# A two-layer mLSTM and attention step on one core: other places for weight sums, norm squares, row masks, sample queries and a last state

## The chip, the cores and the metric

The kernel runs on one core of a Trainium2 chip. Its time is the device time of one execution in microseconds (us), and of several runs the median counts. The engines are named PE (TensorE), DVE (VectorE), ACT (ScalarE), POOL (GpSimd) and SP (SyncE, which only issues DMAs here).

## The reference

One inference step of a decoder of two layers over 16 meta rows and 1024 prompt rows, and over 8 samples of 8 rows, with the same weights. Layer 0 mixes by an mLSTM recurrence (8 heads, chunks), layer 1 by an attention with forget gates that reads one shared K and V (for the samples, 4 pages of cache each as well). Cut to what matters:

```python
def run_trunk(h, C0, n0, m0, lead, attend, prm):
    for l in range(2):
        if l == 0:
            a, (C, n, m) = mlstm_mixer(rmsnorm(h, norm_a), C0, n0, m0, lead, w_in_a, ..., w_out_a)
        else:
            a = fox_mixer(rmsnorm(h, norm_b), shared, attend, w_qo_b, q_norm_b, w_out_b)
        h = h + a
        h = h + swiglu(rmsnorm(h, norm_ffn[l]), w_gate_up[l], w_down[l])
        if l == 0:
            shared = shared_kv(h, norm_kv, w_kvf, b_fg_b, k_norm_b)   # k, v, log forget values
    return rmsnorm(h, norm_final), C, n, m, shared

def mlstm_mixer(...):          # p = xn @ w_in: q, k, v, output gate, two gate columns a head
    lf = log_sigmoid(softcap(gf + b_fg))
    h, state = mlstm_sequence(q, k, v, li, lf, state0, lead)         # C: 64x128 a head, n: 64
    return (rmsnorm(h, mh_g) * sigmoid(og)) @ w_out, state

def swiglu(xn, w_gu, w_d):     # D_FF = 2816
    gu = xn @ w_gu
    return (silu(gu[..., :D_FF]) * gu[..., D_FF:]) @ w_d
```

The outputs are y of both groups, the last C, n and m, and the new k, v and log forget values. D_MODEL is 1024 and everything is float32.

## The kernel before

The 1104 rows (80 of samples and meta rows, 1024 of the prompt) lie along the free dimension in four pieces (TS, 276 rows each) or three (TT: 336, 384, 384); the model dimension lies on the partitions, in 8 blocks (KT). A float32 product is three fp32r products of a high and a low part (`mm3`, L189 to L191). The high part is a cast on ACT, the low part a difference on DVE: L261 and L262, or L255 and L256 where a gain is multiplied in, L249 and L250 in the first phase.

The program runs in this order. **phase_a** makes queries, keys, values and gates of the mLSTM. In its loop over the query and key products (mmA), the gates' log-sigmoid is taken (a chain of DVE steps, L269 to L280) and turned by TensorE (rps, L880, from lf_tm); stg holds a product until it is stored to qkD, and wo_out splits w_out into whi and wlo and stores them to woD. **The recurrence** goes over 9 chunks; behind the last, `last_state` stores C and n (out_p_C, out_p_n) and `norm_heads` takes the heads' norm from squares that ACT sums up (jk, L1228). **mlp** of layer 0 makes the output projection in units (pops, L512; `unit(t, m, x)` does 128 columns for row piece t), among which `gate` turns the normed heads and multiplies them by the output gates loaded from ogD (ghps and ogc, L1314 and L1315). **ffn** makes gate and up products of pairs of column blocks by a seven-product scheme (m1 to m7 of 2x2 blocks; L1369 the products, L1350 and L1375 the additions that combine them). `PairWeights` makes the weights' sums (L82 to L85) and splits them, `TwoNorms` the row pieces' sums and their high and low parts (T?A_ and T?B_, L104). The down projection (dps, L1701) follows in rounds, with the row pieces' norms for what comes next. **first_values** and **phase_b** make K, V, the forget values and the layer 1 queries (tmps, bps, btp); `attend_sample`, `attend_prompt`, **mlp** of layer 1 and the last norm follow.

A norm of a row piece is made in four steps. `square` (ACT, L328) adds block after block into sq, on POOL or, for the last ones, on DVE (L333). `root` sums over the partitions on TensorE (nps, L341) and takes the root on ACT (L344). `diag` takes the reciprocal and puts it on a diagonal (DVE, L350 and L352). `spread` multiplies by ones on TensorE (nps, L359) and copies out on ACT (L360). The products of the last blocks are in the list of sums and not in one tile.

What sets the order: on the engines named in a `manual_schedule` instructions run as the program writes them, on the others a tile scheduler places them. PE is fixed in the query and key loop; PE, DVE, ACT and POOL in the recurrence; PE, DVE and ACT from output unit 1 on, through the start of ffn up to `order.close()`; PE, DVE and ACT in the loop over the later column blocks; PE alone in the down projection and the sample attention. phase_b is placed by the scheduler. `Q` is a list of jobs with a cost each; `tick(x)` runs the next ones for x us of room, `tick(99)` all of them:

```python
def go(x, h, *names):
    for y in names:
        getattr(x, y)(h)           # the product
        getattr(x, y + "_out")(h)  # its additions
        tick(1.0)
```

A tile is taken from a pool under a tag; a tag has one or more buffers, and the next tile of a tag waits until the oldest is free. jk of the recurrence has two, and so have bhi and blo (the high and low parts of the turned queries, stored to qDh and qDl). The sample attention (`turn`: ktp, kT; `score`: sps, from kT and the block-diagonal queries qb) begins while output gates (bps, og2D) are still made. qmt are the meta rows' queries, built in the same way (L2319 and L2323). Row masks (L2113 to L2118) are 128 partitions by 8 or 16 columns, NEG away from a diagonal of blocks: POOL sets and cuts the copies in a scratch tile (tag rm, one buffer), DVE takes their maximum (qi and q8, mi and m16).

Of the kernel before, what the change touches and what calls it, by code (L numbers as in the profile page):

```python
# [17 lines left out]
P = 128  # L18
D = 1024
# [74 lines left out]
class TwoNorms:  # L94
# [69 lines left out]
    def jobs(self):  # L164

        return [(2.0, lambda: self.scaled(range(4))), (2.0, lambda: self.scaled(range(4, 8))), (1.3, self.first),
                (1.3, self.second_a), (1.5, self.second_b), (1.3, self.second_c), (1.5, self.second_d)]

    def late_jobs(self):
        return [(1.5, self.third), (1.3, self.third_b), (1.3, self.fourth), (1.3, self.fifth)]  # L170


class Net:
# [19 lines left out]
    def consts(self):  # L193
# [12 lines left out]
        self.clast = c.tile([P, 1], F32, name="clast")  # L206
        with self.pool("g0") as gp, self.pool("g0p", space=PSUM) as pp:
# [85 lines left out]
    def tm_proj(self, pieces, g, pp, tag, bufs, evac, then=None):  # L293
# [3 lines left out]
        parts = [  # L297
            self.load_w([p[a * P : b * P] for p in pieces], None if g is None else g + a, nk=b - a)
            for a, b in zip(ks, ks[1:])
        ]  # L300
# [17 lines left out]
    def add_sq(self, H, t, m, sp, x, late=KT - 1):  # L318
# [3 lines left out]
        n = t1 - t0  # L322
        if x == 0:
# [91 lines left out]
    def run(self):  # L415
# [4 lines left out]
        self.Q = []  # L420
# [30 lines left out]
    def mlp(self, H, raws, w, l, heads=None, cb=None):  # L451
# [5 lines left out]
        with self.pool(self.uid("nsp")) as sp, self.pool(self.uid("npp"), bufs=2, space=PSUM) as pn:  # L457
# [14 lines left out]
            with ExitStack() as c:  # L472
# [60 lines left out]
                for m in range(KT):  # L533
                    unit(0, m, m)
                    gate(1) or gate(2)
# [111 lines left out]
def phase_a(self, vt):  # L647
# [5 lines left out]
    with ExitStack() as c3:  # L653
# [59 lines left out]
        with self.pool("rowsA") as rp, self.pool("rowsAp", bufs=2, space=PSUM) as rpp, \  # L713
# [220 lines left out]
def recurrence(self, kp, rec, v, qkD, fill, gate):  # L934
# [12 lines left out]
    with ExitStack() as cr, self.pool("recAp", bufs=2, space=PSUM) as pp:  # L947
# [28 lines left out]
        with self.pool("rec2") as sets[2], self.pool("rec1", bufs=2) as rp, self.pool("rec3") as sets[0]:  # L976
# [8 lines left out]
            for i in range(1, NT):  # L985
# [11 lines left out]
                if i == NT - 1:  # L997
                    self.last_state(C[i % 2])
# [21 lines left out]
def last_state(self, C):  # L1020
# [300 lines left out]
def ffn(self, H, l, weights, order, TA, pn, pair, each, early, end=None):  # L1321
# [14 lines left out]
    with self.pool(f"ffn{l}") as fp, self.pool(f"ffnp{l}", space=PSUM) as pp:  # L1336
# [197 lines left out]
        Q += [(1.3, lambda: weights.split(1, 0, a1)), (2.2, lambda: weights.sums(1, nc.vector))]  # L1534
# [3 lines left out]
        n.diag()  # L1538
        go(g, 0, "m7")
# [12 lines left out]
        n.third()  # L1552
# [3 lines left out]
        n.third_b()  # L1556
# [7 lines left out]
        weights.split_sums(1, 0)  # L1564
        weights.sums(2)
# [9 lines left out]

        weights.split(2, 0)
        u.do("m7", "m5")
# [222 lines left out]
def first_values(self, H, pp, pn):  # L1800
# [3 lines left out]
    halves = self.vhalves  # L1804
    for tiles in ((0, 1), (5,), (2, 3), (4,), (6, 7), (8,)):
        vs = self.ny(f"vf{tiles[0]}").rearrange("p k t -> p (k t)")[:, :512].rearrange("p (i d) -> p i d", i=2)
        for z, i in enumerate(tiles):
# [14 lines left out]
            elif i == 1:  # L1822
                self.diag(st)
                self.tick(2.0)
# [869 lines left out]
```

## Time and profile before

| | |
|---|---|
| time, median of 3 runs | 2888.94 us (2888.35 to 2890.04) |
| profiled execution | 2890.53 us: a span of 2887.8 us and 2.7 us around it |
| mean granted TensorE clock | 0.988 |
| busy | PE 97%, PEld 93%, DVE 61%, ACT 40%, POOL 29% of the span |
| DMA | 469.42 MB, mean 163 GB/s |

Times in views of the trace count from the start of the span. A row of the timeline has the start, the busy time (of a group of like instructions, with xcount), the engine, the line, the operation, the tile written and the tiles read, and in brackets the idle time ahead of it with what ended it. A row of the waits has the waiting engine, its line and tile, what it waited for, and then the total in us, the number of times and the longest. A row of the stretches has from and to, the length, the busy time of PE, PEld, DVE, ACT and POOL each with its number of instructions, the granted clock (1.00 is full), the DMA engines' busy share and GB/s.

### The profile page before, as it was taken

What the parts mean: (1) busy time and instruction counts of PE and PEld (TensorE: products, weight loads), DVE (VectorE), ACT (ScalarE), POOL (GpSimd) and SP (SyncE); (2) the same over time, 40 slices, a digit from 0 to 9 for tenths busy, and PEclk for the clock granted to TensorE, in tenths of its full rate; (3) what the DMA queues carried; (4) which work ended last, traced back from release to release, by engine and by line L of the source; (5) the groups of instructions that cost most, each with busy time, mean ns of one, the idle gap of its engine ahead of it and who ended that gap; (6) DMA issues with size and microseconds to landing.
All of it is one profiled execution on the core that took longest, in us unless ns stands there. A gap on an engine that the chain in (4) does not pass through costs nothing. (4 is left out here: it accounts for less than half of the span.)

```text
span 2887.8 us, 60472 instructions
## 1 busy us (share of the span) xinstructions
PE 2789.8 (97%) x23601; PEld 2674.4 (93%) x23601; DVE 1773.3 (61%) x3905; ACT 1166.5 (40%) x2288; POOL 836.3 (29%) x1299
## 2 busy tenths in 40 slices
PE   7999989999999999999999999999999999999998
PEld 7999879999999999998999888777899999999998
DVE  5142555788887656563354443677468888866557
ACT  5232463433232334343344454777433232333345
POOL 2021233223233322124353201445332232232111
PEclk9999999999999999999999999999999999999999
DMA  6374546245555375544444676444423555526557
GB/s 197 103 220 124 144 142 229 74 132 166 176 164 158 105 233 176 182 152 132 130 165 139 200 279 238 162 138 134 139 75 104 176 162 175 171 83 220 188 190 227
DMA packets 427255, 469.42 MB, mean 163 GB/s; under 512 B 42114, under 2 KB 352506, under 8 KB 425946
## 3 DMA queue, kind: packets, MB, share of 16 engines
q1 hardware_dynamic: 380066, 317.04, 35.4%
q0 software_dynamic: 44496, 147.07, 15.8%
q8 instruction: 185, 3.03, 0.4%
q10 hardware_dynamic: 2408, 1.46, 0.2%
q14 instruction: 100, 0.82, 0.1%
HBM read 318.25 MB, written 147.21 MB: 161 GB/s over the span
## 5 line engine op out<-in xcount | busy, mean ns | idle before, releaser
L1369 PE MATMUL m<-xh,slot 128*128 128x276 f32 x2752 | 540.6, 290 | 1.2 <-ACT fs L1398 1.2
L1369 PEld LDWEIGHTS m<-xh,slot 128*128 128x128 f32 x2752 | 439.5, 188 | 3.2 <-ACT fs L1398 1.9
L1369 PE MATMUL m<-xl,slot 128*128 128x276 f32 x1376 | 397.2, 289 | 0.2
L1369 PEld LDWEIGHTS m<-xl,slot 128*128 128x128 f32 x1376 | 258.7, 188 | 0.6 <-DVE xl L104 0.6
L190 PE MATMUL tmps<-slot,xh 128*128 128x256 f32 (+2 forms) x864 | 243.4, 282 | 4.5 <-DVE slot L256 4.5
L189 PE MATMUL tmps<-slot,xh 128*128 128x256 f32 (+2 forms) x864 | 245.9, 285 | 0.0
L191 PE MATMUL tmps<-slot,xl 128*128 128x256 f32 (+2 forms) x864 | 243.3, 282 | 0.0
L262 DVE TENSOR_TENSOR slot<-slot,slot 128x1024 fp32r<-128x1024 f32 x124 | 162.7, 1313 | 62.7 <-ACT slot L261 61.2
L261 ACT CAST slot<-slot 128x1024 fp32r<-128x1024 f32 x124 | 129.5, 1045 | 130.0 <-PE m L1369 109.8
L190 PEld LDWEIGHTS tmps<-slot,xh 128*128 128x128 f32 (+1 forms) x864 | 160.6, 186 | 5.0 <-DVE slot L256 4.7
L191 PEld LDWEIGHTS tmps<-slot,xl 128*128 128x128 f32 (+1 forms) x864 | 160.9, 186 | 0.0
L189 PEld LDWEIGHTS tmps<-slot,xh 128*128 128x128 f32 (+1 forms) x864 | 160.1, 185 | 0.2
L189 PE MATMUL mmA<-xh,whi 128*128 128x384 f32 (+1 forms) x384 | 134.1, 349 | 0.1
L191 PE MATMUL mmA<-xh,wlo 128*128 128x384 f32 (+1 forms) x384 | 127.2, 331 | 0.0
L190 PE MATMUL mmA<-xl,whi 128*128 128x384 f32 (+1 forms) x384 | 127.2, 331 | 0.0
L262 DVE TENSOR_TENSOR slot<-vA,slot 128x1024 fp32r<-128x1024 f32 (+1 forms) x59 | 81.5, 1385 | 33.9 <-ACT slot L261 32.8
L262 DVE TENSOR_TENSOR slot<-Ht,slot 128x1024 fp32r<-128x1024 f32 (+1 forms) x59 | 81.3, 1380 | 33.9 <-ACT slot L261 32.8
L250 DVE TENSOR_TENSOR wlo<-wraw,whi 128x1024 fp32r<-128x1024 f32 (+1 forms) x32 | 39.0, 1226 | 100.5 <-ACT whi L249 76.9
L261 ACT CAST slot<-vA 128x1024 fp32r<-128x1024 f32 (+1 forms) x59 | 60.8, 1035 | 97.9 <-PE m L1369 92.1
L261 ACT CAST slot<-Ht 128x1024 fp32r<-128x1024 f32 (+1 forms) x59 | 60.8, 1036 | 97.7 <-PE m L1369 91.5
L1473 DVE TENSOR_TENSOR ws<-ws 128x128 f32<-128x128 f32 x264 | 93.7, 355 | 8.9
L2516 ACT ACTIVATE s<-s,nb 128x272 f32<-128x272 f32 (+7 forms) x126 | 98.8, 786 | 0.0
(755 smaller groups left out, 8711.7 us busy)
## 6 DMA issues: line engine op xcount, KB each, us to landing
ws<-in_w_down SPq DMA_DIRECT2D x176, 128.0 KB
sD<-ws SPq DMA_DIRECT2D x176, 128.0 KB
slot<-sD SPq DMA_DIRECT2D x40, 512.0 KB
slot<-in_w_gate_up SPq DMA_DIRECT2D x36, 512.0 KB
kp<-in_cache_k SPq DMA_DIRECT2D x32, 512.0 KB
vp<-in_cache_v SPq DMA_DIRECT2D x32, 512.0 KB
vA<-in_w_gate_up SPq DMA_DIRECT2D x26, 512.0 KB
Ht<-in_w_gate_up SPq DMA_DIRECT2D x26, 512.0 KB
```

The source lines that it names most:

```text
L189: mm(ps, sh, mh, start=first, stop=False)
L190: mm(ps, sh, ml, start=False, stop=False)
L191: mm(ps, sl, mh, start=False, stop=last)
L250: low = lambda: nc.vector.tensor_tensor(out=lo, in0=raw, in1=hi.bitcast(F32), op=ALU.subtract)
L261: self.nc.scalar.copy(hi, src)
L262: self.nc.vector.tensor_tensor(out=lo, in0=src, in1=hi.bitcast(F32), op=ALU.subtract)
L1369: nc.tensor.matmul(u.ps[h, b], w[p][:, k], x[q][:, k], start=first and k == i == 0, stop=k == 3 and i == 2, skip_group_check=True)
L1473: tt(out=o, in0=a, in1=b, op=ALU.subtract)
L2516: nc.scalar.activation(ss[z, u], ss[z, u], AF.Exp, bias=nb[:, z : z + 1], accum_out=sm[:, u, z : z + 1])
```

## The change

- **Weight sums behind the diagonal.** In `ffn`, the sums of the second pair of weights are queued behind `n.diag()`; the steps third_a and third_b of `TwoNorms` become jobs, and what is left comes in another order; the splits and sums of later weights stand behind the products m7 and m5 of the next unit.
- **Squares added one step later.** The DVE addition of a square is kept in `owed` until the next square or the root.
- **Row masks early.** Both masks are made in the query and key loop of phase_a, into one constant tile, rowm.
- **Third weight part early.** The third part of the last value columns' weights is made among the row tiles 6 and 7 of `first_values`.
- **Sample queries at once.** qtS and ktS are loaded on POOL's queue right behind the last store of qS and kS; all block-diagonal copies are DVE's; og0s (the first output gates) moves from the buffer of whi to one of bhi.
- **Last state turned.** n is copied (nnP), transposed by TensorE (nnpP), copied again (noP) and stored in rows; in the first output unit, the number of gates at each of the eight steps goes from one each to 0, 1, 1, 1, 2, 1, 1, 1.

```diff
class TwoNorms:
-    def third(self):
+    def third_a(self):
         for z, t in enumerate(self.t2):
             ks = slice(4 + 2 * z, 6 + 2 * z)
             self.sub(self.y1[:, ks], self.y1[:, ks], t)
-        self.net.nc.scalar.copy(self.T[4][0], self.y1[:, self.hi])
...
+    def third_c(self):
+        self.net.nc.scalar.copy(self.T[4][0], self.y1[:, self.hi])
...
         return [(2.0, lambda: self.scaled(range(4))), (2.0, lambda: self.scaled(range(4, 8))), (1.3, self.first),
-                (1.3, self.second_a), (1.5, self.second_b), (1.3, self.second_c), (1.5, self.second_d)]
+                (1.3, self.second_a), (1.5, self.second_b), (1.3, self.second_c), (1.5, self.second_d),
+                (1.5, self.third_a), (1.3, self.third_b)]
 
     def late_jobs(self):
-        return [(1.5, self.third), (1.3, self.third_b), (1.3, self.fourth), (1.3, self.fifth)]
+        return [(0.0, self.third_c), (1.3, self.fifth), (1.3, self.fourth)]

Net.consts:
+        rm = c.tile([P, P], F32, name="rowm")
+        self.q8, self.m16 = rm[:, :NQ], rm[:, NQ : NQ + NM]

Net.tm_proj (the weight parts are made by the new tm_weights, as functions):
+    def tm_proj(self, pieces, g, pp, tag, bufs, evac, then=None, parts=()):
+        ks, todo = self.tm_weights(pieces, g)
+        parts = [*parts, *(f() for f in todo[len(parts) :])]

Net.square and Net.root:
+        self.settle()
...
-        (nc.vector if x >= late else nc.gpsimd).tensor_tensor(out=s, in0=s, in1=sq, op=ALU.add)
+        if x >= late:
+            self.owed.append(lambda: nc.vector.tensor_tensor(out=s, in0=s, in1=sq, op=ALU.add))
+        else:
+            nc.gpsimd.tensor_tensor(out=s, in0=s, in1=sq, op=ALU.add)
+
+    def settle(self):
+        while self.owed:
+            self.owed.pop()()
 
     def root(self, t, pp, **kw):
+        self.settle()

mlp, first output unit:
                     unit(0, m, m)
-                    gate(1) or gate(2)
+                    for _ in range((0, 1, 1, 1, 2, 1, 1, 1)[m]):
+                        gate(1) or gate(2)

phase_a, loop over the query and key products:
+                if x == 12:
+                    for n, out in ((NQ, self.q8), (NM, self.m16)):
+                        self.row_mask(rp.tile([P, P // n, n], F32, name=self.uid("rm"), tag="rm"), out, n)

last_state:
-        nc.gpsimd.dma_start(O["p_n"][0, 0, a::2].rearrange("j k -> k j").unsqueeze(2), cs[:, :, DV:])
+    n = rp.tile([P, DV], F32, name="nnP", tag="jk")
+    nc.vector.tensor_copy(n[:, :4], C[:, :, DV])
+    ps = pp.tile([P, P], F32, name="nnpP", tag="cps")
+    nc.tensor.transpose(ps[:4, :], n[:, :4], self.ident)
+    no = rp.tile([P, DV], F32, name="noP", tag="jk")
+    nc.vector.tensor_copy(no[:4], ps[:4])
+    nc.gpsimd.dma_start(O["p_n"][0, 0].rearrange("(j a) k -> j a k", a=2), no[:4].rearrange("p (a k) -> p a k", a=2))

ffn:
-        Q += [(1.3, lambda: weights.split(1, 0, a1)), (2.2, lambda: weights.sums(1, nc.vector))]
+        Q += [(1.3, lambda: weights.split(1, 0, a1))]
         go(g, 0, "m1", "m6")
         n.root()
         go(g, 0, "m2")
         n.diag()
+        Q += [(2.2, lambda: weights.sums(1, nc.vector))]
...
         g.m7(1)
-        n.third()
+        n.third_c()
         g.m6(1)
         g.m6_out(1)
         g.m7_out(1)
-        n.third_b()
         n.fourth()
...
         go(g, 1, "m3")
-        weights.split_sums(1, 0)
-        weights.sums(2)
         weights.load(3)
...
+        u.do("m7")
+        weights.split_sums(1, 0)
+        weights.sums(2)
+        u.do("m5")
         weights.split(2, 0)
-        u.do("m7", "m5")

first_values:
+    todo, self.v3 = self.tm_weights([self.I["w_kvf"][:, D + 768 : D + 1040]], G_KV)[1], []
...
+            elif i in (6, 7):
+                self.v3.append(todo.pop(0)())

phase_b (and parts=self.v3 in the call of tm_proj for c == 3):
+        self.qkS = [sk.tile([P, 8, T0], F32, name=n) for n in ("qtS", "ktS")]
...
                             nc.gpsimd.dma_start(dstS[f], st)
+                            if f == 7:
+                                nc.gpsimd.dma_start(self.qkS[1 - gi], dstS.rearrange("m p t -> p m t"))
...
-        s = w7.tile([P, KT * P], F32R, name="og0s", tag="whi", bufs=1).bitcast(F32)
+        s = fp.tile([P, GL], F32R, name="og0s", tag="bhi").bitcast(F32)

attend_sample (its two row masks and its loads of qtS and ktS are gone):
-                (nc.vector if b else nc.gpsimd).tensor_copy(Q[r, u::2, c : c + NQ], qt[r, u::2, b * NQ : (b + 1) * NQ])
+                nc.vector.tensor_copy(Q[r, u::2, c : c + NQ], qt[r, u::2, b * NQ : (b + 1) * NQ])
```

The change moves instructions at many places; here are three on VectorE. The lines in the rows of the kernel after are its own, up to 36 higher than before's for the same step.

In the query and key loop of phase_a (lsz, lsq and lsw belong to the log-sigmoid), VectorE before:

```order
L271 TENSOR_SCALAR lsz_1945<-lse_1944 128x72
L272 RECIPROCAL lsz_1945<-lsz_1945 128x72
L273 TENSOR_TENSOR lsz_1945<-lsz_1945,lse_1944 128x72
L274 TENSOR_TENSOR lsq_1946<-lsz_1945 128x72
L275 TENSOR_SCALAR lsw_1947<-lsq_1946 128x72
```

And after:

```order
L276 TENSOR_SCALAR lsz_1946<-lse_1945 128x72
L2151 TENSOR_REDUCE rowm<-rm_2488 128x8
L277 RECIPROCAL lsz_1946<-lsz_1946 128x72
L2151 TENSOR_REDUCE rowm<-rm_2602 128x16
L278 TENSOR_TENSOR lsz_1946<-lsz_1946,lse_1945 128x72
L279 TENSOR_TENSOR lsq_1947<-lsz_1946 128x72
```

Both masks' reduces now stand between two steps of the chain that ends in lf_tm.

In the start of layer 0's ffn (ws are the down weights' sums, fs and vA products and normed rows), VectorE before, from the second T0B part on:

```order
L104 TENSOR_TENSOR T0B_2l<-t_383_6138,T0B_2h 128x552
L1350 TENSOR_TENSOR ws_0_6291<-ws_0_6291 128x128
L1473 TENSOR_TENSOR ws_0_6291<-ws_0_6291 128x128 x3
L1375 TENSOR_TENSOR vA<-m_385_6158,vA 128x276
L104 TENSOR_TENSOR vA<-vA,t_382_6137 128x552
L104 TENSOR_TENSOR vA<-vA,t_383_6138 128x552
L1350 TENSOR_TENSOR fs_5978<-fs_5978,m_387_6218 128x276
L1350 TENSOR_TENSOR vA<-fs_5978,m_386_6202 128x276
L104 TENSOR_TENSOR T0B_1l<-vA,T0B_1h 128x1104
L104 TENSOR_TENSOR T0B_4l<-vA,T0B_4h 128x1104
```

And after:

```order
L104 TENSOR_TENSOR T0B_2l<-t_385_6316,T0B_2h 128x552
L104 TENSOR_TENSOR vA<-vA,t_384_6315 128x552
L104 TENSOR_TENSOR vA<-vA,t_385_6316 128x552
L1378 TENSOR_TENSOR ws_0_6463<-ws_0_6463 128x128
L1501 TENSOR_TENSOR ws_0_6463<-ws_0_6463 128x128 x2
L1403 TENSOR_TENSOR vA<-m_387_6336,vA 128x276
L104 TENSOR_TENSOR T0B_1l<-vA,T0B_1h 128x1104
L1501 TENSOR_TENSOR ws_0_6463<-ws_0_6463 128x128
L1378 TENSOR_TENSOR ws_1_6466<-ws_1_6466 128x128
L1501 TENSOR_TENSOR ws_1_6466<-ws_1_6466 128x128 x3
L1378 TENSOR_TENSOR fs_6156<-fs_6156,m_389_6397 128x276
L104 TENSOR_TENSOR T0B_4l<-vA,T0B_4h 128x1104
```

T0B_1l moves up by two additions of products; T0B_4l moves behind the sums of the down weights of both blocks.

At the start of the sample attention, VectorE before, from the last blo of the queries on:

```order
L1959 SCALAR_TENSOR_TENSOR blo_18236<-btp_18231,gqk,bhi_18235 128x384
L256 SCALAR_TENSOR_TENSOR wlo_19405<-slot_4749,gain,whi_19404 128x128 x8
L2201 COPY kT_18263<-ktp_18307 128x512
L2201 COPY kT_18264<-ktp_18326 128x512
L2190 COPY qb_14780<-qtS 64x4x8 x4
L2323 COPY qmt_20196<-qtS 64x16 x8
```

And after:

```order
L2217 COPY qb_14786<-qtS 64x4x8 x4
L261 SCALAR_TENSOR_TENSOR slot_4934<-slot_4926,gain,slot_4930 128x128 x8
L261 SCALAR_TENSOR_TENSOR wlo_19409<-slot_4927,gain,whi_19408 128x128 x2
L1993 SCALAR_TENSOR_TENSOR blo_18234<-btp_18229,gqk,bhi_18233 128x384
L261 SCALAR_TENSOR_TENSOR wlo_19409<-slot_4927,gain,whi_19408 128x128 x6
L1993 SCALAR_TENSOR_TENSOR blo_18244<-btp_18239,gqk,bhi_18243 128x384
L2350 COPY qmt_20200<-qtS 64x16 x8
L2228 COPY kT_18267<-ktp_18311 128x512
L2228 COPY kT_18268<-ktp_18330 128x512
```

The qb copies and the split of wlo move ahead of the last blo, and the qmt copies ahead of the first kT.

More of the change, by code (lines that the diff above doesn't have):

```diff
@@ L291, in fm_cols, with tm_weights @@
             self.mm3(ps, wh[:, k, :], wl[:, k, :], xh[:, k, :], xl[:, k, :], k == 0, k == KT - 1)
-    def tm_proj(self, pieces, g, pp, tag, bufs, evac, then=None):
+    def tm_weights(self, pieces, g):
         n = sum(p.shape[1] for p in pieces)
         ks = (0, 4, 8) if n <= 256 or not self.slots else (0, 3, 6, 8)
[L297 to L300, printed above, removed]
+        make = lambda a, b: self.load_w([p[a * P : b * P] for p in pieces], None if g is None else g + a, nk=b - a)
+        return ks, [(lambda a=a, b=b: make(a, b)) for a, b in zip(ks, ks[1:])]
+    def tm_proj(self, pieces, g, pp, tag, bufs, evac, then=None, parts=()):
+        n = sum(p.shape[1] for p in pieces)
+        ks, todo = self.tm_weights(pieces, g)
+        parts = [*parts, *(f() for f in todo[len(parts) :])]
         at = [(w, k) for w, a, b in zip(parts, ks, ks[1:]) for k in range(b - a)]
@@ L419, in run @@
         self.slots = None
-        self.Q = []
+        self.Q, self.owed = [], []
         cy, cb = ExitStack(), ExitStack()
@@ L2098, in sample_prep @@
     nc.gpsimd.memset(ncn, NEG)
-    q8 = sp.tile([P, NQ], F32, name="q8")
-    qi = sp.tile([P, HB, NQ], F32, name="qi", tag="rm")
-    self.row_mask(qi, q8, NQ)
     for b in range(NB):
-        nc.vector.tensor_tensor(out=ncn[:, b, b * NQ : (b + 1) * NQ], in0=cnew[:, b, :], in1=q8, op=ALU.add)
+        nc.vector.tensor_tensor(out=ncn[:, b, b * NQ : (b + 1) * NQ], in0=cnew[:, b, :], in1=self.q8, op=ALU.add)
     return cq, ncn
@@ L2161, in attend_sample @@
     dm, m16, qb = masks
-    qt = sp.tile([P, 8, T0], F32, name="qtS")
-    kt = sp.tile([P, 8, T0], F32, name="ktS")
-    for t, d in ((qt, self.qS), (kt, self.kS)):
-        (nc.scalar if t is qt else nc.gpsimd).dma_start(t, d.rearrange("m p t -> p m t"))
+    qt, kt = self.qkS
     vn = sp.tile([NS, D], F32, name="vnS")
```

12 lines of the change are left out of this document (5 added, 7 removed).

## The prediction

> **What bounds the kernel now.** I read the page's busy times first, then the list of who waited for whom on TensorE, then the granted clock stretch by stretch, and last the timelines around the lines that the change touches.
>
> ```profile
> span 2887.8 us, 60472 instructions
> PE 2789.8 (97%) x23601; PEld 2674.4 (93%) x23601; DVE 1773.3 (61%) x3905; ACT 1166.5 (40%) x2288; POOL 836.3 (29%) x1299
> ```
>
> TensorE is busy 2789.8 of 2887.8 us, so 98 us of idle time are all that better ordering can win, with what a low clock stretches. VectorE (61%) and GpSimd (29%) have room on average, and the edits move their work only. So the question at each edit is which of TensorE's waits ends earlier. The list of TensorE's waits (total us, times, longest) names them:
>
> ```profile
> PE nps L359 <- DVE sq L352: 9.6, 5, 2.1
> PE ghps L1314 <- DVE ogc L1315: 4.7, 2, 4.2
> PE tmps L190 <- DVE slot L256: 4.5, 1, 4.5
> PE sps L2209 <- POOL qb L2190: 3.1, 1, 3.1
> PE ktp L2200 <- DVE kT L2201: 2.8, 1, 2.8
> PE m L1369 <- DVE T0B_1l L104: 2.1, 1, 2.1
> PE m L1369 <- DVE T1B_1l L104: 2.1, 1, 2.1
> PE m L1369 <- DVE vA L1350: 2.0, 1, 2.0
> PE m L1369 <- DVE Ht L1350: 2.0, 1, 2.0
> ```
>
> These rows hold 32.9 us. Each sits at a place where the diff reorders the engine named behind the arrow. A second cost is the clock; in the table by stretches it is the number behind the POOL column:
>
> ```profile
> 456.20:459.60 3.40, 3.22 (x15) 3.22 (x15) 2.24 (x6) 1.46 (x3) 1.34 (x2) 0.50 1.02 410
> 562.00:565.40 3.40, 3.40 (x17) 3.40 (x17) 1.76 (x4) 0.67 (x2) 0.00 (x0) 0.50 0.44 131
> 1282.20:1292.50 10.30, 8.39 (x37) 7.77 (x38) 5.05 (x13) 3.59 (x9) 2.62 (x3) 0.50 0.68 223
> 1323.20:1330.00 6.80, 5.30 (x24) 5.30 (x25) 2.83 (x8) 0.00 (x0) 4.21 (x13) 0.50 0.70 213
> 1633.80:1637.20 3.40, 3.05 (x13) 3.05 (x14) 0.98 (x2) 0.74 (x2) 0.00 (x0) 0.50 1.08 247
> 1640.60:1644.10 3.50, 3.33 (x24) 2.83 (x25) 1.39 (x9) 0.00 (x0) 1.27 (x4) 0.51 1.02 409
> 2158.00:2200.00 42.00, 35.25 (x270) 34.12 (x271) 34.81 (x56) 17.37 (x27) 6.22 (x5) 1.00 0.27 80
> ```
>
> Behind waits of 1.9 to 4.5 us come stretches of 3.4 us or a small multiple at a clock of 0.50, in which half of TensorE's busy time is lost: (3.2 + 3.4 + 8.4 + 5.3 + 3.1 + 3.3) / 2 = 13.3 us in these six. The last row, the FFN start of layer 1, holds the same waits as layer 0's and stayed at 1.00, so a wait does not always bring one.
>
> **The change part by part.** Gains are +, losses -.
>
> *Row masks in phase A.* Timelines of GpSimd and VectorE at the masks' old place, then of the log-sigmoid chain and TensorE at the new one (start, us):
>
> ```profile
> 1310.12 0.62 POOL L2113 MEMSET qi<- 128x8 f32 x16
> 1310.69 2.21 POOL L2114 TENSOR_SCALAR_AFFINE_SELECT qi<-qi 128x8 f32<-128x8 f32 x15
> 1321.24 1.28 POOL L2114 TENSOR_SCALAR_AFFINE_SELECT mi<-mi 128x16 f32<-128x16 f32 x8
> 1323.81 0.37 DVE L2118 TENSOR_REDUCE m<-mi 128x16 f32<-128x128 f32 x1 [6.83 <-POOL mi L2116]
> ...
> 151.08 0.54 POOL L710 DMA_DIRECT2D qkD<-stg  x1 [1.53 <-ACT stg L709]
> 153.22 0.23 DVE L273 TENSOR_TENSOR lsz<-lsz,lse 128x72 f32<-128x72 f32 x1
> 159.66 0.23 DVE L280 SCALAR_TENSOR_TENSOR lf_tm<-lf_tm,lsw 128x72 f32<-128x72 f32 x1
> 163.49 0.78 PE L880 MATMUL rps<-ident,lf_tm 80*8 80x80 f32 x6
> ```
>
> The order puts the masks behind the store at 151.08 and both reduces inside the chain from L273 to L280. The first mask takes 0.62 and two passes of 16 selects (15 took 2.21), 0.62 + 4.7 = 5.3 us, to 156.9; its reduce, taken as 0.4, ends at 157.3; the second takes 0.3 (half the memsets) + 2 x 1.28 = 2.9, and its reduce (0.37) ends at 160.6. L273, the first step behind both, starts then instead of at 153.22; what follows took 159.89 - 153.22 = 6.7, less 0.8 in which a weight was waited for. lf_tm is ready at 166.5, TensorE comes for it at 163.49: **-3.0** (0 if the scheduler's order leaves GpSimd earlier than I place it, -5 with a half-clock stretch). Queued behind the masks on GpSimd are stores of queries and weights, which TensorE reads much later.
>
> *The last state's n, turned by TensorE.* Two stores of single elements go; a transpose is put into TensorE's queue ahead of the first output unit. Its input copy takes a buffer of the tag of the squares' scratch, which the seventh of the eight squares must have left:
>
> ```profile
> 437.19 0.58 PE L189 MATMUL pops<-xh,wo 128*128 128x276 f32 x1
> 440.42 0.30 ACT L1228 ACTIVATE jk<-vA 128x128 f32<-128x128 f32 x1
> ```
>
> 440.42 is that seventh square. With its end (440.72) and a copy as short as the 0.23 steps above, the transpose starts at about 441.0, where before the unit's matmuls started at 437.19: -3.8. Against it stand the two waits for ogc, 4.7: the gates come one unit later, TensorE itself comes 3.8 later, and the two stores no longer lie ahead of the gates' load. **+0.9** (-3.8 if ogc is late anyway, +4.7 if the transpose finds its input).
>
> *FFN start, both layers.* The weight sums are four steps of 0.69:
>
> ```profile
> 557.83 0.69 DVE L82 TENSOR_TENSOR vA<-slot 128x512 f32<-128x512 f32 x1
> 583.09 1.30 DVE L104 TENSOR_TENSOR T0B_4l<-vA,T0B_4h 128x1104 fp32r<-128x1104 f32 x1
> ```
>
> They stood ahead of the reciprocal and diagonal (L350, L352); behind them 2.8 us are taken from a wait of 1.9, which goes. The T1 and T2 parts are made as jobs under TensorE's products, so the waits of 2.1 for T?B_1l go; the products' additions no longer stand behind the splits and sums of later weights, so those of 2.0 (vA, Ht) go. What is late next is T?B_4l: its step (1.30) now stands behind the third and fifth steps and the sums of the down weights, and its product comes sooner by what is saved. I charge 1.3, its own length, in each layer. 2 x (1.9 + 2.1 + 2.0 - 1.3) = **+9.4** (between +3, where T?B_4l takes half of it, and +12).
>
> *Squares one step later in the down projection.* Waits of TensorE around the first two, then around the third, of layer 0's norms:
>
> ```profile
> PE nps L359 <- DVE sq L352: 3.8, 2, 2.1
> PE nps L341 <- DVE vA L1350: 0.8, 1, 0.8
> ...
> PE nps L359 <- DVE sq L352: 1.9, 1, 1.9
> PE nps L341 <- DVE vA L1350: 1.4, 1, 1.4
> ```
>
> VectorE now adds a square only when the next is due, so the residual's additions do not queue behind a ScalarE square. The first root and diagonal, 0.8 + 2.1, and the third, 1.4 + 1.9, are freed; the second diagonal (3.8 - 2.1 = 1.7) waits for a cast behind a load and stays. Of 6.2 I leave 1.2 for the sum that is still owed at the root: **+5.0** (0 to +6.2).
>
> *Third weight part of the last value columns.* TensorE's wait of 4.5 (tmps <- slot) is VectorE's split, which stood behind the mask reduce at 1323.81. Parts are now made two tiles earlier and the reduce is gone: **+4.0**, 0.5 left for the third part, whose raw data reuse a buffer (-2 if that load comes late, +4.5).
>
> *Sample start.*
>
> ```profile
> 1615.28 0.54 POOL L1967 DMA_DIRECT2D qS<-bst  x1
> 1626.54 0.55 POOL L1995 DMA_DIRECT2D og2D<-og0s  x1 [2.62 <-ACT og0s L1994]
> 1631.10 2.40 DVE L256 SCALAR_TENSOR_TENSOR wlo<-slot,gain,whi 128x128 fp32r<-128x128 f32 x8 [2.70 <-ACT whi L255]
> 1634.15 1.97 PE L2200 MATMUL ktp<-ident,kp 128*128 128x128 f32 x8 [2.78 <-DVE kT L2201]
> 1640.11 0.75 POOL L2190 COPY qb<-qtS 64x32 f32<-64x32 f32 x4 [8.29 <-DMA qtS<-qS]
> 1641.95 1.45 DVE L2323 COPY qmt<-qtS 64x16 f32<-64x16 f32 x8 [1.31 <-POOL qmt L2319]
> ```
>
> The transposed queries are loaded behind the last qS store (1615.28) instead of in the sample's own start, so the 3.1 for qb goes. The 2.8 for kT does not: og0s now holds a buffer of the bhi pair until its store lands (about 1630.7, where the whi casts that waited for it let VectorE on), the last bhi cast waits for it, and VectorE has the eight qmt copies (1.45, behind GpSimd's memset) ahead of kT. I put kT 1.5 later than before: 3.1 - 1.5 = **+1.6** (-3 if the qb copies, too, block VectorE on their load; +5.9 if both waits go).
>
> *Sum.* -3.0 + 0.9 + 9.4 + 5.0 + 4.0 + 1.6 = **17.9 us** of waits. For the clock: of the 13.3 us I leave the two at the sample start (1.5 + 1.7), since the wait for kT stays, and half of the 4.2 at 1282, a long stretch of which only one end hangs on the freed waits; the new waits of 3.0 and 3.8 may bring a stretch of 1.7 each. 13.3 - 3.2 - 2.1 - 3.4 = **4.6**. Together 22.5: from the profiled execution's 2890.5 (its span and 2.7 around it) to 2868.0. The median, 2888.94, is 1.6 lower than that execution; since the terms are this coarse, I keep **2868**.
>
> The rule of the Trainium skill, "TensorE: Matmul & The Clock Gate", Part 1 (HAM oscillation), is that idle gaps of TensorE over some 3.4 us throttle it, with a free-running window of 3.4 us. The window's length fits the 3.40 rows; the threshold does not: the stretches at 562.0 and 1633.8 follow waits of 1.9 and 2.8. It becomes a rival below.
>
> **The rivals.**
>
> *A. The waits go as summed and the clock comes back (above), 2868.* Chance 0.48.
>
> *B. Only a wait as long as a whole stretch costs clock.* Then the clock comes back only behind the 4.2 (3.2 / 2) and the 4.5 (5.3 / 2), 4.3 us, and the new 3.8 costs 1.7: 17.9 + 4.3 - 1.7 = 20.5, 2870. For it: layer 1 at 1.00 behind 2-us waits. Against it: 562.0 and 1633.8. The Trainium skill's page named above states this. Chance 0.12.
>
> *C. What is late next takes half.* TensorE reaches the next operand earlier by what it saved, and VectorE, at 34.81 of 42 us in the FFN start, is itself nearly full: T?B_4l takes 3 in each layer, the down projection's norms give only the roots (2.2 of 5.0), the sample start 0: 17.9 - 3.4 - 2.8 - 1.6 = 10.1, clock 0, 2880. Chance 0.22.
>
> *D. The changed orders do not reach the waits.* The row masks and the transpose cost 6.8 as worked out, the FFN and the norms gain as much: no change, 2889. Against it: five waits for L352 end in VectorE rows that the diff moves. Chance 0.08.
>
> *E. Slower: GpSimd's queue is held at the early loads.* Each of the two loads (keys, queries) makes GpSimd wait until the stores just issued have landed, and the stores of qDh and qDl, which free VectorE's and ScalarE's buffers, are queued behind it. TensorE's next transposes come some 5 us after the store at 1615.28 is issued; a landing of L us stalls it L - 5, twice, and brings a long stretch (8.4 / 2 = 4.2) each time. To eat 22.5 and 5.8 more, L must be 15. The load of qtS shows 8.29 of waiting on GpSimd in the sample start, under a DMA share of 1.02 to 1.08; at 1615 a store would have to take twice that. At 18 us: 2868 + 2 x 13 + 8.4 = 2902. Chance 0.10.
>
> **How the numbers follow.** About 0.2% (5.8 us) can be told from no change. A, B and C are faster, 0.82; D is the same, 0.08; E slower, 0.10. The range goes from the optimistic ends of the FFN start, the sample start and the transpose (2.6 + 4.3 + 3.8 = 10.7, to 2857) up to C with both unlike terms failing, 2884; outside it lie D and E and a rest.
>
> **What would show it.** Right: no wait of over 0.5 at nps <- sq in the FFN starts and at tmps <- slot; none at sps <- qb; a new one of about 3 at rps <- lf_tm near 163 and of about 3.8 at the transpose near 441; clock 1.00 around 562 and 1323. Wrong: T?B_4l waits of over 2, a wait for ogc that stays, a clock of 0.5 at stretches that had 1.00, or GpSimd idle for over 5 us in front of the qtS load.

## The result, and the profile after

| | before | after |
|---|---|---|
| median | 2888.64 us (2880.49 to 2890.04, 4 runs) | 2866.50 us (2865.79 to 2867.38, 4 runs) |
| ratio | | 0.9929, 95% interval 0.9911 to 0.9948 |
| profiled execution | 2890.53 us | 2865.79 us |

The change is faster by 0.7%, 22 us; 2868 was forecast. Measured again later, after took 2866.3.

The page of after, its first lines:

```profile
span 2864.1 us, 60485 instructions
PE 2774.5 (97%) x23602; PEld 2660.8 (93%) x23602; DVE 1770.8 (62%) x3911; ACT 1165.3 (41%) x2288; POOL 835.1 (29%) x1295
```

The span fell by 23.7 us. Only 8.4 of them are idle time of TensorE (2887.8 - 2789.8 = 98.0 before, 89.6 now); 15.3 are busy time, with one matmul more. The same matmuls take less time mostly because less of them lies at half clock (priced below). TensorE's waits at the touched places, after:

```profile
PE ktp L2227 <- DVE kT L2228: 6.6, 1, 6.6
PE nps L377 <- DVE sq L370: 6.3, 3, 4.7
PE nnpP L1051 <- DVE nnP L1049: 3.5, 1, 3.5
PE m L1397 <- ACT fs L1426: 3.3, 2, 1.6
PE rps L902 <- DVE lf_tm L285: 2.9, 1, 2.9
PE mmA L192 <- ACT stg L728: 1.9, 1, 1.9
PE m L1397 <- DVE slot L267: 1.6, 2, 0.8
PE m L1397 <- DVE T1B_4l L104: 0.6, 1, 0.6
PE m L1397 <- DVE T0B_4l L104: 0.6, 1, 0.6
```

The waits for ogc (4.7), slot at tmps (4.5), qb (3.1), T?B_1l (2.1 twice) and the two of 2.0 are gone from the list. So are those of 1.9 at nps in the two FFN starts. New are nnpP, rps, mmA, slot (a weight split, 0.8 in each FFN start) and the T?B_4l; the wait for kT has grown from 2.8 to 6.6, that for fs from 1.2 to 3.3, and the wait of the second norm's nps from 1.7 to 4.7.

Stretches of after, the clock again behind the POOL column:

```profile
165.29:172.12 6.83, 6.01 (x23) 5.24 (x24) 2.51 (x10) 1.36 (x3) 0.55 (x1) 0.50 0.55 195
438.36:452.01 13.65, 9.49 (x42) 8.24 (x43) 8.13 (x22) 7.11 (x26) 3.31 (x6) 0.50 0.81 295
545.00:602.00 57.00, 54.79 (x432) 54.26 (x431) 49.54 (x82) 25.42 (x39) 10.48 (x12) 1.00 0.29 87
1270.00:1290.00 20.00, 19.22 (x165) 18.86 (x164) 12.46 (x33) 7.71 (x21) 4.99 (x8) 1.00 0.52 171
1300.00:1320.00 20.00, 20.00 (x166) 20.00 (x165) 5.57 (x12) 7.81 (x23) 11.54 (x28) 1.00 0.68 225
1615.96:1622.79 6.83, 4.54 (x30) 3.98 (x30) 2.80 (x10) 0.58 (x1) 0.45 (x1) 0.50 0.78 240
```

The FFN start, the third norm and the value columns (rows three to five) are free of half clock. The masks' new place, the transpose and the sample start each have a stretch of 6.8 us or more; of these three, only the masks' new place had none in before.

The starts of the same TensorE instruction in both traces, subtracted, show where the time went. Each row is the change between one such place and the next:

| from one place to the next, start in before's and in after's trace | change, us |
|---|---|
| log-sigmoid in phase A: 100.71 / 100.53 to 172.96 / 179.78 | +7.0 |
| last chunk and output unit 0, to 459.60 / 464.19 | -2.2 |
| output units, to 529.47 / 535.09 | +1.0 |
| FFN start of layer 0, to 611.97 / 611.09 | -6.5 |
| FFN loop, to 1200.44 / 1198.60 | -1.0 |
| first two norms of the down projection, to 1216.83 / 1213.09 | -1.9 |
| third norm, to 1292.16 / 1281.71 | -6.7 |
| value columns, to 1329.99 / 1312.35 | -7.2 |
| rest of phase_b, to 1555.08 / 1536.03 | -1.4 |
| sample start, to 1643.22 / 1623.77 | -0.4 |
| attention, to 1800.65 / 1779.57 | -1.6 |
| up to layer 1's FFN and its start, to 2213.26 / 2187.91 | -4.3 |
| the rest, to 2852.58 / 2828.52 | +1.3 |

Not every row repeats. In a second profiled execution of after (the run after_again below), the row of the last chunk is 4.0 us longer, that of the attention 1.5 longer and that up to layer 1's FFN 2.7 shorter, all others within 0.5. What these three rows show cannot be put down to the edits by this table alone.

### The profile page after: what moved, and what is told of

It reads as the page before. It is cut to its first block, busy times and chain, and to the rows that moved or that the text cites. A ratio compares the mean times of both kernels' runs of the same rounds, so it can differ in the third digit from the quotient of the medians.

```text
span 2864.1 us, 60485 instructions
## 1 busy us (share of the span) xinstructions
PE 2774.5 (97%) x23602; PEld 2660.8 (93%) x23602; DVE 1770.8 (62%) x3911; ACT 1165.3 (41%) x2288; POOL 835.1 (29%) x1295
```

## The experiments

The first seven undo one part of the change in the kernel after; two put one part alone into the kernel before; two look for a better order; one is after once more. Before, measured beside them, had medians of 2889.4 to 2890.3. Totals of one kernel spread by up to 13 us from execution to execution (before: 2881.6 to 2894.5 in 19 runs), so a verdict of a few us rests on the waits and not on the total alone. Waits and starts are those of the one profiled execution of each kernel.

**u_masks**, the masks back at their old place:

```diff
-                if x == 12:
-                    for n, out in ((NQ, self.q8), (NM, self.m16)):
-                        self.row_mask(rp.tile(...), out, n)
+    qi = sp.tile([P, HB, NQ], F32, name="qi", tag="rm")
+    self.row_mask(qi, self.q8, NQ)
+    mi = sp.tile([P, P // NM, NM], F32, name="mi", tag="rm")
+    self.row_mask(mi, self.m16, NM)
```

> The kernel after, with both row masks back at their old place in the sample attention; the third weight part stays early. After's median is 2866.5. Theory 1 (either edit alone frees the value columns' weights): phase A gets back what it lost there between the 100th and the 175th us, 7.0, and the wait of 4.5 at tmps stays away, since the splits now stand ahead of the reduces: 2859.5. Theory 2 (the wait goes only with both edits): 7.0 come back in phase A, but 7.2 return around 1320 with a half-clock stretch: 2866.7. In both the waits of rps for lf_tm (2.9) and of mmA for stg (1.9) are gone.

2859.5 us (2855.8 to 2860.3). Theory 1: phase A gets its time back (the rps that started at 166.11 starts at 162.07, the mmA at 179.78 starts at 171.65), and TensorE waits for nothing between 1290 and 1320. Next to the early weight parts the early masks bring nothing and cost 7 us.

**u_v3**, the third weight part at its old place:

```diff
-            elif i in (6, 7):
-                self.v3.append(todo.pop(0)())
```

> The kernel after, with the third weight part of the last value columns made at its old place; the row masks stay early. Theory 1 (either edit alone frees the value columns' weights: VectorE was held by the mask reduces): no change, 2866.5, no wait over 1 at tmps for slot. Theory 2 (the parts had to be made earlier): the 4.5 and a half-clock stretch return, 2872 to 2874.

2869.2 us (2868.2 to 2869.5). The wait at tmps stays away, so the masks' leaving is enough as well; the 7.2 do not return. Of the 2.7 above after, 0.7 is seen in the third norm (1.5 at nps for sq instead of 0.8) and 1.4 in a wait at the very end (fin for Ht, 3.2 instead of 1.8) that comes and goes between executions.

**b_masks** and **b_v3** put the two into the kernel before, one at a time:

```diff
 b_masks: before with (and without the two masks in the sample attention)
+                if x == 12:
+                    for n, out in ((NQ, self.q8), (NM, self.m16)):
+                        self.row_mask(rp.tile(...), out, n)
 b_v3: before with (and parts=self.v3 in tm_proj)
+            elif i in (6, 7):
+                self.v3.append(todo.pop(0)())
```

> The kernel before, with the row masks alone built early in phase A. Its median is 2889 to 2890. Theory 1 (the mask reduces alone held VectorE in front of the value columns' weights): phase A loses 7.0, the wait of 4.5 at tmps goes with its half-clock stretch, 7.2: no change, 2889.5. Theory 2 (the wait is that of late weight parts): the wait stays, 2896.

> The kernel before, with the third weight part alone made early; the masks stay in the sample attention. Theory 1 (either edit alone frees the wait of 4.5 at tmps): 2882. Theory 2 (VectorE is held by the reduces, and the scheduler now puts the splits of the third part behind them, so the part comes no sooner): the wait stays at 4 to 8, 2889 to 2893.

b_masks took 2889.8 us, ratio 1.0000 (0.9988 to 1.0012): theory 1, loss and gain cancel. By the starts of the same instructions, phase A loses 7.0, the value columns gain 5.3 of their 7.2, and the third norm, which the theory left out, 2.3. b_v3 took 2889.0, ratio 1.0004 (0.9993 to 1.0014): theory 2. TensorE's waits at these places, of b_masks and then of b_v3:

```profile
PE rps L885 <- DVE lf_tm L282: 2.9, 1, 2.9
PE mmA L189 <- ACT stg L711: 2.8, 1, 2.8
PE tmps L190 <- DVE slot L258: 0.6, 1, 0.6
```

```profile
PE tmps L190 <- DVE gqk L1906: 6.1, 1, 6.1
```

VectorE of b_v3 there, the two mask reduces and the splits behind the second:

```profile
1309.94 0.40 DVE L2126 TENSOR_REDUCE q<-qi 128x8 f32<-128x128 f32 x1 [6.11 <-POOL qi L2124]
1317.35 0.36 DVE L2126 TENSOR_REDUCE m<-mi 128x16 f32<-128x128 f32 x1 [5.97 <-POOL mi L2124]
1318.11 2.14 DVE L256 SCALAR_TENSOR_TENSOR slot<-slot,gain,slot 128x272 fp32r<-128x272 f32 x5
```

With the masks early, tmps waits 0.6; with the parts alone early, 6.1, more than before, since VectorE's order has the splits of the part behind the mask reduces. In u_masks the scheduler put the reduces behind the splits of these parts (the first reduce starts at 1309.59, the last of the 272-column splits at 1299.67). So what freed the value columns is that splits and reduces stand the right way round on VectorE, by whichever edit.

**u_turn** and **u_gates** undo the halves of the last state's edit:

```diff
 u_turn: the copies and the transpose replaced by
+        nc.gpsimd.dma_start(O["p_n"][0, 0, a::2].rearrange("j k -> k j").unsqueeze(2), cs[:, :, DV:])
 u_gates:
-                    for _ in range((0, 1, 1, 1, 2, 1, 1, 1)[m]):
-                        gate(1) or gate(2)
+                    gate(1) or gate(2)
```

> The kernel after, with the last state's n stored by single elements again and no transpose; the new numbers of gates stay. Theory 1 (the gates' numbers remove the waits for ogc): the transpose's wait of 3.5 and 0.9 of low clock go and nothing returns, 2862. Theory 2 (the element stores on GpSimd's queue delay the load of ogc, so the transpose paid for itself): a wait for ogc of 3 to 4 returns, 2865 to 2867.

> The kernel after, with one gate at each of the eight steps of the first output unit again; the transpose stays. Theory 1 (the gates' numbers remove the waits for ogc): waits of TensorE for ogc of 3 to 5 return, 2870. Theory 2 (the transpose alone does, by coming 3.5 later and by taking the element stores away): wait for ogc under 1, 2866.5.

u_turn: 2864.9 us (2860.6 to 2870.6), too wide to judge by. Its trace has the wait for ogc back at 1.5, and the places behind unit 0 come 2.4 us earlier by after's measure (from 4.8 late ahead of the transpose to 2.3 late at 466): between the two theories. But after's second profiled execution is 4.0 later than its first at that place, so one trace does not price the transpose. u_gates: 2868.8 (2862.3 to 2872.2), too wide as well, and its trace has no wait for ogc at all: theory 2 by the waits, the numbers of gates do nothing beside the transpose. What the pair shows is which waits come and go; what the edit is worth in time stays open.

**u_ffn**, the FFN start as before:

```diff
-        Q += [(1.3, lambda: weights.split(1, 0, a1))]
+        Q += [(1.3, lambda: weights.split(1, 0, a1)), (2.2, lambda: weights.sums(1, nc.vector))]
...
-        n.third_c()
+        n.third()
...
+        n.third_b()
...
+        weights.split_sums(1, 0)
+        weights.sums(2)
         weights.load(3)
```

> The kernel after, with the FFN start as before: the sums of the second weight pair ahead of the diagonal, the third steps in one piece, the splits and sums of later weights ahead of m7. Theory 1 (the FFN start gave 5.5 and 4.3 in the two layers, and nothing takes it up later): 2876.3; the waits of 1.9 (nps for sq), 2.1 (T?B_1l) and 2.0 (vA and Ht) return in each layer. Rival (the loop over the later column blocks takes the difference up): 2869 or less at the same waits.

2875.1 us (2871.6 to 2876.8): theory 1, 8.6 longer. Its waits in layer 1's FFN start:

```profile
PE m L1394 <- DVE T1B_1l L104: 2.1, 1, 2.1
PE m L1394 <- DVE Ht L1375: 2.0, 1, 2.0
PE nps L374 <- DVE sq L367: 0.9, 1, 0.9
PE m L1394 <- ACT fs L1423: 0.6, 1, 0.6
```

Two waits return in full. The third, nps for sq, returns at 0.9 instead of 1.9: the squares one step later, which this kernel keeps, are the likely taker of the other half (u_squares, below, loses 0.7 in each FFN start). In return after's waits there for slot (0.8) and T?B_4l (0.6) are gone, and that for fs is 0.6 instead of 1.6. Between the same places each FFN start is 4.2 us longer than after's (5.5 and 4.3 forecast), and the later loop takes up nothing.

**u_squares**, each square added at once:

```diff
-            self.owed.append(lambda: nc.vector.tensor_tensor(out=s, in0=s, in1=sq, op=ALU.add))
+            nc.vector.tensor_tensor(out=s, in0=s, in1=sq, op=ALU.add)
```

> The kernel after, with each late square added on VectorE at once. Theory 1 (the addition one step later frees VectorE in the down projection: 2.9 around 1200 and 6.7 around 1280, low clock with it): 2876. Rival (the 6.7 around 1280 came from the third weight part, which no longer stands between VectorE's additions there): only the 2.9 and what the next load leaves of it return, 2867 to 2870, and the third norm's waits stay under 1.

2872.6 us (2868.5 to 2875.2), between the two. Its waits in the first two norms, then in the third:

```profile
PE nps L377 <- DVE sq L370: 4.4, 2, 2.5
PE nps L359 <- DVE vA L1378: 0.8, 1, 0.8
...
PE nps L377 <- DVE sq L370: 1.9, 1, 1.9
PE nps L359 <- DVE vA L1378: 0.8, 1, 0.8
```

The rival is wrong, the third norm's waits return to 1.9 and 0.8. Theory 1 is too large: by the starts of the same instructions each of the two places gives back 2.5, not 2.9 and 6.7. The rest of the 6.7 is before's stretch of 10.3 us at half clock there, which this execution does not have. It is the fastest of the four (2868.5), so the 6.1 by which the median is longer is not resolved by it.

**u_sample**, the sample start as before:

```diff
-        self.qkS = [sk.tile([P, 8, T0], F32, name=n) for n in ("qtS", "ktS")]
...
-        s = fp.tile([P, GL], F32R, name="og0s", tag="bhi").bitcast(F32)
+        s = w7.tile([P, KT * P], F32R, name="og0s", tag="whi", bufs=1).bitcast(F32)
...
+    qt = sp.tile([P, 8, T0], F32, name="qtS")
+    kt = sp.tile([P, 8, T0], F32, name="ktS")
```

> The kernel after, with the sample start as before: qtS and ktS loaded in the sample attention, og0s in the buffer of whi, GpSimd copying the first qb. Theory 1 (the wait for kT, 6.6 after and 2.8 before, eats what the wait for qb, 3.1, gave): 2866.5 within 1.5. Rival (the early loads gain, and the 6.6 is only a different place for the same landing): the wait for qb returns on top, 2869 to 2870.

2873.1 us (2870.3 to 2875.7), which neither theory gives, and by the starts not because of the sample start, which is 1.8 us shorter than after's: 3.9 us are lost in the value columns and 2.7 in the last chunk, whose time varies. The first two rows stand at the sample start; the third lies 300 us earlier:

```profile
PE ktp L2227 <- DVE kT L2228: 4.7, 1, 4.7
PE sps L2236 <- POOL qb L2217: 0.8, 1, 0.8
...
PE tmps L193 <- DVE slot L261: 1.8, 1, 1.8
```

At the start itself the old way waits 5.5 in all, 1.1 less than after's 6.6. At the new wait at tmps, this trace has the loads of the key and query gains ahead of a weight cast on ScalarE (issued from 1304.3 to 1307.4, the cast at 1307.74), after's has them behind: another choice of the scheduler. Its waits at the start are not before's either (2.8 and 3.1), though the three edits are undone. By itself the early load of the sample queries is not shown to gain, and the total cannot say.

**better** moves three places:

```diff
 masks, in cache_prep instead of the query and key loop:
         nc.gpsimd.memset(on, 1.0)
+        for n, out in ((NQ, self.q8), (NM, self.m16)):
+            self.row_mask(sp.tile([P, P // n, n], F32, name=self.uid("rm"), tag="rm"), out, n)
 last state, ahead of the last chunk's output instead of behind it:
+                if i == NT - 1:
+                    self.last_state(C[i % 2], pp, rp)
                 self.chunk_out(i, R, rp, *args, den, ssq, g, exp=N2 and N2["exp"])
 first output gates:
-        s = fp.tile([P, GL], F32R, name="og0s", tag="bhi").bitcast(F32)
+        s = fp.tile([P, GL], F32R, name="og0s", tag="og0s", bufs=1).bitcast(F32)
```

> The kernel after with three places moved: the masks built around the 46th us, where GpSimd idles until the 80th; the last state's n copied and transposed ahead of the last chunk's output, right behind its state, so that it waits for no square; og0s in a buffer of its own. Theory 1 (the three losses are local): the 7.0 of phase A, the 4.4 at the transpose and some 4 of the 6.6 at kT come back, 15 in all: 2851. Rival (other waits take their place: the waits for ogc return when TensorE comes 3.5 earlier, and GpSimd's or VectorE's work at 46 us delays the first products): 2858 to 2862.

2848.4 us (2846.2 to 2851.3), ratio to before 0.9851 (0.9830 to 0.9872): theory 1, and 3 more. The waits of rps for lf_tm and of mmA for stg are gone from its list, and that of ktp for kT is 0.3. Between the same places phase A gains 7.2 on after and the sample start 8.8, of which 3.6 go again in the attention; the last chunk and unit 0 gain 3.0, although the transpose waits longer (below), but that row varies by as much between executions of after.

**best2** leaves the transpose where after has it and only copies early:

```diff
+                if i == NT - 1:
+                    n = rp.tile([P, 4], F32, name="nnP", tag="nn", bufs=1)
+                    nc.vector.tensor_copy(n, C[i % 2][:, :, DV])
                 self.chunk_out(i, R, rp, *args, den, ssq, g, exp=N2 and N2["exp"])
```

> The kernel called better, with one thing changed: the copy of the last state's n stays right behind the state, but its transpose stands on TensorE where it stands after, ahead of the first output unit, so it waits neither for the square nor for the state. If the wait of 5.9 that better has at the transpose is its own, it goes, and 2 to 4 us with it: 2844 to 2846. If it only takes the place of waits for the gates around it (ogeb 2.4, ogqk 1.5 after), they come back: 2848.

2851.5 us (2850.3 to 2852.6): the second case. TensorE's waits from 425 to 470, of better and then of best2:

```profile
PE nnpP L1050 <- DVE nnP L1048: 5.9, 1, 5.9
PE ghps L1341 <- DVE ogc L1342: 1.0, 1, 1.0
```

```profile
PE ghps L1342 <- DVE ogqk L1343: 2.5, 2, 1.3
PE ghps L1342 <- DVE ogeb L1343: 1.9, 1, 1.9
PE nps L1243 <- ACT vA L1213: 0.6, 1, 0.6
```

6.9 against 5.0: the transpose's wait stood mostly in the place of waits for the gates around it. So the total is not longer because of this place. The two profiled executions differ by 5.1 us of span; 2.5 of them are the wait at the very end, which better's has at 0.7 and this one at 3.2, and the rest is not resolved.

**after_again:**

> The kernel after, unchanged, as the base for the kernels of this study in one call with before: 2866.5 within 1.5. The waits of its trace should repeat within 0.3 each; the stretches at half clock need not stand at the same places.

2866.3 us (2865.2 to 2868.9), as expected. The waits at the touched places repeat within 0.3 but for one: that of mmA for stg is 3.7 in all instead of 1.9. So the price of the masks' stores behind that wait varies from execution to execution.

## Why the prediction was right

The total was right to 2 us, and the signs of it came: no wait at nps in the FFN starts, at tmps for slot or at sps for qb, a new one of 2.9 at rps and of 3.5 at the transpose, full clock around 562 and 1323. The split was not right: 17.9 of waits and 4.6 of clock were forecast; idle time gave 8.4 and busy time 15.3. One error of 9.5 and one of 10.7 cancelled, and that is luck. One sign of being wrong came too: half clock at 165, where before had full clock.

| part | waits forecast | waits measured |
|---|---|---|
| masks | -3.0 | -2.9 - 1.9 = -4.8 |
| transpose and gates | +0.9 | 4.7 - 3.5 = +1.2 |
| FFN starts | +9.4 | 12.0 - 1.2 - 2.1 - 1.6 = +7.1 |
| squares | +5.0 | 7.9 - 6.3 = +1.6 |
| third weight part | +4.0 | +4.5 |
| sample start | +1.6 | 5.9 - 6.6 = -0.7 |
| sum | +17.9 | +8.9 |

- **Masks.** The chain of steps was right: lf_tm late by 2.9. The step that failed is "stores of queries and weights, which TensorE reads much later": the stores free stg, ScalarE empties mmA into stg, and TensorE waited 1.9 for it some 14 us later. A half-clock stretch of 6.8 us came on top.

GpSimd and VectorE of after, the masks in their new place:

```profile
154.07 2.34 POOL L2149 TENSOR_SCALAR_AFFINE_SELECT rm<-rm 128x8 f32<-128x8 f32 x16
156.45 0.42 DVE L2151 TENSOR_REDUCE rowm<-rm 128x8 f32<-128x128 f32 x1 [4.24 <-POOL rm L2149]
159.88 0.37 DVE L2151 TENSOR_REDUCE rowm<-rm 128x16 f32<-128x128 f32 x1 [2.50 <-POOL rm L2149]
160.35 0.54 POOL L729 DMA_DIRECT2D qkD<-stg  x1
```

- **Transpose.** Its wait, forecast at 3.8 for the seventh square, was 3.5, and VectorE's row names the square:

```profile
447.28 0.17 DVE L1049 COPY nnP<-C 128x4 f32<-128x4 f32 x1 [1.50 <-ACT jk L1256]
```

- **FFN starts.** The waits named went (2 x 6.0). T?B_4l, charged at 1.3, cost 0.6; what was not seen is TensorE's wait for ScalarE's step for fs, which grew by 1.0 in each layer (1.2 in all before, 3.3 after), and a new one for a weight split on VectorE (slot, 0.8 in each). So 2.4 in each layer was taken back, not 1.3.
- **Squares.** The step that failed is "the second diagonal (1.7) waits for a cast behind a load and stays". It did not stay. Counted from the start of the first spread, TensorE comes 3.1 us earlier (6.3 behind it instead of 9.4), the cast comes when it came (9.3 instead of 9.5), and the wait became 4.7. ScalarE of after:

```profile
1211.42 0.42 ACT L266 CAST T0A_1h<-hr 128x276 fp32r<-128x276 f32 x1 [5.14 <-DMA hr<-hB_1T]
```

- **Third weight part.** The size was right; its owner was not. It was given to the early parts, and in the kernel before those alone free nothing (b_v3); it belongs to the order of splits and reduces.
- **Sample start.** That kT would come later, behind the bhi cast and the qmt copies, was right; 1.5 was too little, it waits 3.8 longer. ScalarE and VectorE of after have the reason: the last bhi cast waits for the store of og0s, as forecast, and behind it the qmt copies wait for GpSimd's memset, which stands behind the stores of that bhi and blo:

```profile
1612.18 0.58 ACT L1992 ACTIVATE bhi<-btp,gqk 128x384 fp32r<-128x384 f32 x1 [2.12 <-DMA og2D<-og0s]
1612.79 0.62 DVE L1993 SCALAR_TENSOR_TENSOR blo<-btp,gqk,bhi 128x384 fp32r<-128x384 f32 x1 [2.27 <-ACT bhi L1992]
1615.95 1.52 DVE L2350 COPY qmt<-qtS 64x16 f32<-64x16 f32 x8 [2.54 <-POOL qmt L2346]
1617.50 0.69 DVE L2228 COPY kT<-ktp 128x512 f32<-128x512 f32 x1
```

- **Clock.** The stretches behind freed waits went nearly all, also the one at 1282 of which half had been left. Summed over the span, time at half clock fell from 69.7 to 46.6 us and TensorE's busy time in it from 59.4 to 33.4; half of that difference, as the forecast counts, is 13.0 us of clock instead of 4.6. The step that failed is that only six of before's stretches were priced: those at 97.8 (3.4), 1207 (6.8) and 1797.6 (3.4) are gone from after's profile too. Not all of that is the change, since after_again has one of 3.4 at 1780.7 again. The other 2.3 of the 15.3 are not resolved.
- **The rivals.** On the waits C was nearer than the forecast: 10.1 in all, against 8.9 in the rows and 8.4 of idle time, and 6.0, 2.2 and 0 for the FFN starts, the norms and the sample start, against 7.1, 1.6 and -0.7. What is late next did take half; C's 2880 failed because it gave the clock nothing. So on the waits the step of the forecast that failed is its charge for what is late next: 1.3 in each FFN start and 1.2 in the norms, where 2.4 and 4.6 were measured. D and E did not come: GpSimd idled 1.82 ahead of the qtS load, not over 5. B gave 2870, near the total, but its rule is refuted in the last section.

## What to carry to other kernels

A wait that goes is worth its length and, where the clock drops behind it, the stretch as well; both have to be counted, and so has the next operand, whose load does not come earlier because the engine does. Work moved into another engine's idle time must be placed where that engine is idle and where nothing in order behind it is waited for: the same masks cost 7 us in the log-sigmoid chain and nothing 100 us earlier. A tile that takes a buffer under a shared tag takes its last user's finish time too: a square for n, a store for the last bhi.

## What the runs showed of the hardware

**Half-clock stretches lie on a fixed grid, and most follow a window of it in which TensorE idled for 1.6 us or more.** In every trace the half-clock stretches start on one grid with a step of 3.413 us and, but for the last, which outlasts the kernel, are one or more steps long. Two windows and their successors, in the kernel before (layer 0, then layer 1, which has the same waits), and in b_masks (layer 1):

```profile
558.61:562.02 3.41, 1.51 (x11) 1.24 (x10) 2.68 (x6) 0.13 (x1) 0.00 (x0) 0.99 0.09 25
562.02:565.43 3.41, 3.41 (x17) 3.41 (x16) 1.76 (x4) 0.65 (x2) 0.00 (x0) 0.51 0.43 129
2159.46:2162.87 3.41, 2.58 (x21) 2.36 (x19) 3.38 (x6) 1.50 (x2) 0.00 (x0) 1.00 0.00 0
2162.87:2166.28 3.41, 2.33 (x17) 2.28 (x18) 2.42 (x7) 0.46 (x2) 0.00 (x0) 1.00 0.51 152
```

```profile
2159.20:2162.61 3.41, 1.51 (x11) 1.23 (x10) 2.38 (x7) 0.39 (x1) 0.00 (x0) 1.00 0.20 58
2162.61:2166.02 3.41, 3.41 (x18) 3.41 (x17) 1.72 (x4) 0.39 (x1) 0.00 (x0) 0.51 0.32 98
```

Where a wait of 1.9 falls whole into one window (1.51 of 3.41 busy), the next runs at half clock; where the grid cuts it in two (2.58 and 2.33 busy), none does. Layer 1 was spared in one execution of before by the grid's position, not by its waits. Counted over the fourteen profiled executions (windows at full clock between the first 40 us and the last 30): of windows with over 2.0 us idle, all 67 were followed by half clock; with 1.6 to 2.0, 16 of 50; with less, 33 of some 11,150. So removing part of a wait can pay more than its length, and the grid's position, which differs between executions of one kernel, is a likely cause of their spread (before's 2881.6 to 2894.5); that was not tested by itself.

Idle time is not the whole of it: 33 of these 116 half-clock stretches began behind windows with less than 1.6 us idle, and in twelve of the fourteen traces one of them follows the window in which TensorE runs most of its products of 8 columns (wps, L926 and L927 in before), with at most 0.2 us idle. In before:

```profile
186.51:189.92 3.41, 3.41 (x22) 3.24 (x23) 0.66 (x3) 1.05 (x1) 0.09 (x1) 1.00 1.11 364
189.92:193.33 3.41, 3.41 (x12) 3.41 (x12) 1.23 (x1) 0.00 (x0) 0.00 (x0) 0.50 0.86 253
```

That narrow products count for less than their time is a guess; no run tests it.

The Trainium skill, "TensorE: Matmul & The Clock Gate", Part 1 (The HAM clock gate), gives a free-running window of 3413 ns; these traces agree. It asks for gaps over some 3.4 us before the clock drops; here 1.9 us sufficed when they lay in one window.
